# Turning the last block's frames on VectorE through memory, and loading and turning the second block's frames earlier

## The chip, the cores and the metric

The kernel runs on one core of one Trainium2 chip. The metric is the device time of one execution in microseconds (us); a kernel's time is the median of several executions. A core has TensorE (PE; its weight loads are PEld), VectorE (DVE), ScalarE (ACT), GpSimd (POOL) and SyncE (SP). SP and POOL issue most transfers between memory and the on-chip buffers, each in the order of its own queue. All engines work through their lists in order; semaphores make one wait for another.

## The reference

One inference step of a streaming encoder with one layer. There are 2048 prompt frames and 32 sample frames, 2080 in all, of width 1024.

```python
hn = rmsnorm(h, g_mix)
proj = hn @ w_in                       # 1024 -> 3072: hA, bA, cA, zA, vB, zB of 512 each
u = cA * hA                            # mixer A: causal convolution of width 3
yA = bA * (conv3(u) + conv_b) * silu(zA)
# mixer B: 4 groups of 128 channels, trailing mean over 2/4/8/16 frames minus the frame
yB = (pooled @ pool_w) * pool_scale * silu(zB)
h = h + concat[yA, yB] @ w_out
h = h + (p @ w_ple) * sigmoid(rmsnorm(h, g_ple) @ w_ple_gate)
y = rmsnorm(h, g_final)                # and the last frames of u and v as states
```

Everything is float32. The kernel splits each factor of a product into a high and a low part in a shorter format and adds three products of parts (high x high, high x low, low x high).

## The kernel before, in words

**Blocks and groups.** The 2080 frames are five blocks of 416 (`NB`), in `GROUPS = [[0, 1], [2, 3], [4]]`. A block has four columns of frames: three of 128 and one of 32. `w_in`'s product needs the frames turned, that is channels on partitions and frames along the row. To get there each column of 128 frames is loaded as rows (`x_load`, on SP, into the ring `xin` of five buffers), its squares are summed on ScalarE (`x_stat`, `sumsq`), the root is taken on POOL, VectorE scales it by the root and by `g_mix` (`normal`, one instruction of 128x1024), TensorE turns it in eight 128x128 pieces, four to a bank (`turn`), and `put`/`split` reads the bank twice: a cast on ScalarE gives the high part, a subtraction on VectorE the low part.

**The beginning.** Block 0 is loaded, turned and split first, into `B0["11"]` and `B0["21"]` (the halves of the channels). Its short column and block 1's are loaded together as `short0`. The weights of the first three products, `zb`, `v` and `c` of the first unit, are loaded and split ahead (`first_w`). Then the generator `second` (`second_block`) does block 1 step by step: three steps that load, sum and scale a column each, four that turn a column, split it into `B0["12"]` and `B0["22"]` and copy the turned frames back over the column's rows (`both`), and four that build sums and differences of the two blocks. The first unit's `Unit.plain` takes these steps between its products: `zb`, `v`, `c` of block 0, then `zb`, `v`, `c` of block 1, then `h`, `za`, `b`. Between them a small product `pm` (`mix`, three matmuls) reads `pw`, the split pooling weights. A turn `pv` puts small vectors (convolution weights, histories, `g_ple`) from `rows` into `vec`; in before it stands ahead of the units. `project` runs a product of 24 matmuls of 128x416, two halves of 12.

**Units 1 to 7.** From the second unit on, two blocks are multiplied together by a scheme of seven block products in place of eight (`Unit.seven`, `pair`): seven steps of 12 matmuls for each of three pairs of weights (`zb`/`v`, `c`/`h`, `za`/`b`). Weights come by SP into `raws` (four buffers) and are split by ScalarE and VectorE into `wr` (seven tiles), ahead of TensorE. During group 0 the generator `next_columns` prepares group 1's frames and writes them to memory (`p_d`). During group 1, from its second unit on, the generator `last_block` prepares block 4: it is taken one step in three calls of `aside`, and there is a call for each step of a pair. Its split frames go through `staged` tiles in `xin` to memory (`b_d`, written by POOL) and are loaded as `hn[4]` at the start of group 2.

**After that.** Group 2 multiplies block 4 plainly. Then come the output projection (`h_d`) and the gate with the final norm, in the same scheme of seven. The gate stage already turns frames on VectorE: `blocks` reads rows of `h_d` so that a 32x32 block transpose over the whole tile (`turned_here`) finishes the turn, and `turned_here`'s result is read through a rearranged view.

**Order.** The list of each engine is set by a scheduler that may move an instruction; `tc.keep_in_program_order` holds one where the program has it. Tiles of a pool are handed out in turn, and a new tile waits until the old one's readers are done. `bank` has six PSUM banks, `tbank` two.

Of the kernel before, what the change touches and what calls it, by code (L numbers as in the profile page):

```python
# [34 lines left out]
def trunk(ctx, tc, x_p, x_s, c_conv, c_pool, p_p, p_s, g_mix, w_in, conv_w, conv_b, pool_w,  # L35
# [19 lines left out]
    def tbank(name):  # L55
        return ps_t.tile([P, 512], F32, tag="tr", name=name)
# [19 lines left out]
    def split(hi, lo, src, eng=nc.vector):  # L76
        ins = nc.scalar.copy(hi, src)  # L77
        eng.tensor_tensor(lo, src, hi.bitcast(F32), op=ALU.subtract)
        return ins
# [227 lines left out]
    def ring4(t, name):  # L307
        return t.tile([P, D], F32, tag="t", name=name)
# [21 lines left out]
    with ExitStack() as s1:  # L330
# [21 lines left out]
        def ftile(name):  # L352
            return wk.tile([P, KH, P], F32, tag="f", bufs=4, name=name)
# [47 lines left out]
        def x_tile(name, rows):  # L401
            return x_stat(x_load(name, rows))

        def normal(x):
            xt, n, r = x
            nc.vector.scalar_tensor_tensor(xt[:n], xt[:n], r[:n], g_bc[:n], op0=ALU.mult, op1=ALU.mult)  # L406

        def turn(x, half, name, get=tbank, later=False):
            xt, n, _ = x
            pt = get(name)  # L410
            for k in range(KH):
                kk = half * KH + k
                ins = nc.tensor.transpose(pt[:, k * P:k * P + n], xt[:n, kk * P:(kk + 1) * P], ident[:n, :n])
# [143 lines left out]
        def half_product(ps, lhs, b, start, stop=True):  # L557

            for k in range(KH):
                for q, (x, y) in enumerate(((0, 0), (0, 1), (1, 0))):  # L560
                    nc.tensor.matmul(ps[:, :NB], lhs[:, k, x], b[:, k, y], start=start and k + q == 0,  # L561
                                     stop=stop and k == KH - 1 and q == 2, skip_group_check=True)

        begun = []

        def project(ps, w, tb):
            x = hn[tb]
            if begun:
                for half in range(2):
                    half_product(ps, w[half], x[half], half == 0, half == 1)  # L570
                return

            begun.append(tb)
            steps = sorted(((k, a, b) for k in range(KC) for a, b in ((0, 0), (0, 1), (1, 0))), key=lambda t: t[1:])
# [12 lines left out]
            for half, q in enumerate(("11", "21")):  # L587
                put(B0[q][:, :, :, c * P:c * P + n], turn(x, half, f"pt0_{c}_{half}", bank)[:, :, :n])
        hn[0] = B0["11"], B0["21"]
        first_w.extend([weights(kind, 0, f"first{kind}") for kind in ("zb", "v", "c")])  # L590
        B0["12"] = piece_of(seventh("B0_12"), 0)
        hn[1] = B0["12"], B0["22"]

        def second_block():

            spans = [(c, slice(c * P, min(NB, c * P + P))) for c in range(4)]
            xs = []
            for c in range(3):
                x = x_tile(f"1_{c}", [x_rows(1, c)])
                normal(x)  # L600
                xs.append((x, slice(0, P)))
                yield
            xs.append((short0, slice(DEC, 2 * DEC)))
            both = []
            for c, cs in spans:
                x, ts = xs[c]
                n = ts.stop - ts.start
                both.append([x[0][:, half * NH:half * NH + KH * n].rearrange("p (k t) -> p k t", k=KH)
                             for half in range(2)])
                for half, q in enumerate(("12", "22")):  # L610
                    pt = turn(x, half, f"pt1_{c}_{half}", bank)[:, :, ts]
                    put(B0[q][:, :, :, cs], pt)
                    nc.scalar.copy(both[c][half], pt)
# [19 lines left out]
        second = second_block()  # L633


        rows = ftile("rows").rearrange("p k n -> p (k n)")[:112, :P]
        nc.gpsimd.memset(rows, 0.0)
        nc.sync.dma_start(rows[0:12], conv_w[0].rearrange("r (j c) -> (r j) c", c=P))
# [2 lines left out]
        nc.sync.dma_start(rows[32:40], c_conv[0, 0].rearrange("r (j c) -> (r j) c", c=P))  # L641
        nc.sync.dma_start(rows[40:100], c_pool[0, 0].rearrange("r (j c) -> (r j) c", c=P))
        nc.sync.dma_start(rows[100:108].rearrange("k (q c) -> k q c", q=4), g_ple[0].rearrange("(q k c) -> k q c", q=4, k=KC))
        pv = tbank("pv")
        nc.tensor.transpose(pv[:, :112], rows, ident[:112, :112])
        vec = const.tile([P, 112], F32, name="vec")
        nc.vector.tensor_copy(vec, pv[:, :112])
        cw = lambda r, j: vec[:, r * 4 + j:r * 4 + j + 1]
        cb = lambda j: vec[:, 12 + j:13 + j]
        pscale = lambda j: vec[:, 16 + j:17 + j]  # L650
        hist_u = lambda j: vec[:, 32:40].rearrange("p (r j) -> p r j", j=4)[:, :, j]
        hist_v = lambda j: vec[:, 40:100].rearrange("p (r j) -> p r j", j=4)[:, :, j]

        pw = one.tile([P, 2, 4, P], F32R, name="pw")
        pw_raw = raws.tile([P, 4, P], F32, tag="t", name="raw_pw")
        nc.sync.dma_start(pw_raw, pool_w[0].rearrange("g c d -> c g d"))
        split(pw[:, 0], pw[:, 1], pw_raw)

        def etile(name, n=NB):
            return wk.tile([P, 2 * NB + 16], F32, tag="e", bufs=2, name=name)[:, :n]  # L660
# [1 line left out]
        class Unit:  # L662
# [98 lines left out]
            def plain(self):  # L761
                tbs, j, tag, zs, V, U, c_s = self.tbs, self.j, self.tag, self.zs, self.V, self.U, self.c_s
                blocks = range(len(tbs))

                def product_of(kind, b, w):
                    ps = bank(f"{kind}{tag}_{tbs[b]}")
                    project(ps, w, tbs[b])
                    return ps[:, :NB]

                def zb_block(b):  # L770
# [5 lines left out]
                        nc.scalar.copy(self.place(V, 15, seg), ps[:, seg[0] - o:seg[1] - o])  # L776
                    self.pool_blocks(b)

                def c_block(b):
                    nc.scalar.copy(self.cols(c_s, b), product_of("c", b, wc))  # L780

                wz, wv = weights("zb", j, f"zb{tag}"), weights("v", j, f"v{tag}")
                if len(tbs) > 1:

                    wc = weights("c", j, f"c{tag}")
                    for b in blocks:
                        zb_block(b)
                        if b == 0:
                            for _ in range(2):
                                next(second)  # L790
                        v_block(b)
                        if b:
                            self.mix(b - 1)
                            next(second)
                        else:
                            for _ in range(2):
                                next(second)
                        c_block(b)
                        if b == 0:
                            for _ in range(3):  # L800
# [242 lines left out]
        def last_block():  # L1043

            load_ahead(2, 0)
            for c in range(4):
                x = x_stat(ahead.pop((2, c))[0], True)
                if c < 3:
                    load_ahead(2, c + 1)
                normal(x)  # L1050
                yield
                for half in range(2):
                    pt = turn(x, half, f"pt4_{c}_{half}", later=True)
                    to_memory(b_d[:, half * KH:half * KH + KH], f"b_4_{c}_{half}", pt, c * P, x[1])
                    yield

        def at_pace(steps, num, den):

# [485 lines left out]
```

## Time and profile before

| what | before |
|---|---|
| runs (us) | 933.43, 933.67, 933.95; median 933.67 |
| the profiled execution (us) | 933.61 |
| its span, first to last instruction (us) | 931.8 |
| TensorE busy | 910.5 us, 98% |
| VectorE busy | 718.9 us, 77% |
| ScalarE busy | 475.3 us, 51% |
| POOL busy | 147.1 us, 16% |
| granted TensorE clock | 0.996 |

A row of a timeline has the start in us from the span's start, the duration in us, the engine, the line of the kernel, the operation, what is written from what, and in brackets how long the engine had been idle and who released it. A row with x12 stands for twelve instructions, and its duration reaches from the first's start to the last's end. Matmuls overlap, so start to start is the measure of what one costs. In a row of a group stand the busy time, the mean of one instruction in ns, and the idle time before. A row of the waits says who waited for whom, in total, how often, and the longest.

### The profile page before, as it was taken

The page shows a single profiled execution, that of the slowest core. Times are in us where ns is not written, and L with a number is a line of the kernel's source. Part 1 is how long each engine was busy: PE and PEld are TensorE (multiplying, and loading weights), DVE is VectorE, ACT ScalarE, POOL GpSimd, SP SyncE. Part 2 cuts the span into 40 slices and gives each one's busy share as a digit, 9 for nine tenths or more (in the row PEclk, how much of TensorE's full clock was granted, in tenths as well). Part 3 has the DMA queues.
Part 4 walks back from the last instruction along what each step waited for, and adds up shares of the span by engine and source line. Part 5 has one row for each costly group of instructions (what it writes and reads, how often), then busy time and mean ns, then how long its engine had stood idle before and what let it go on. Part 6 is the DMA issues. An engine that isn't in the chain of part 4 may idle for free. (4 is left out here: it accounts for less than half of the span.)

```text
span 931.8 us, 12938 instructions
## 1 busy us (share of the span) xinstructions
PE 910.5 (98%) x4511; PEld 821.3 (88%) x4511; DVE 718.9 (77%) x1209; ACT 475.3 (51%) x880; POOL 147.1 (16%) x272
## 2 busy tenths in 40 slices
PE   7999999999999999999999999999999999999996
PEld 5899998999999999999999987888877868888884
DVE  6896898899588978685777588766554798888865
ACT  5744555564445554443554356434424875565554
POOL 2210222212000110000000011111111002323334
PEclk9999999999999999999999999999999999999999
DMA  8255555759954645428655349765784885899892
GB/s 253 75 153 152 166 161 175 239 160 305 417 166 137 182 147 158 139 59 283 200 168 176 119 162 315 265 204 153 244 231 156 304 276 140 199 225 232 211 255 92
DMA packets 138254, 182.96 MB, mean 196 GB/s; under 512 B 11724, under 2 KB 109260, under 8 KB 136909
## 3 DMA queue, kind: packets, MB, share of 16 engines
q1 hardware_dynamic: 118173, 124.36, 43.5%
q0 software_dynamic: 17280, 52.27, 19.4%
q10 hardware_dynamic: 2736, 5.51, 1.8%
q8 instruction: 35, 0.57, 0.3%
q14 instruction: 30, 0.25, 0.1%
HBM read 127.23 MB, written 54.86 MB: 195 GB/s over the span
## 5 line engine op out<-in xcount | busy, mean ns | idle before, releaser
L77 ACT CAST y_S<-y_fS 128x512 fp32r<-128x512 f32 x32 | 19.5, 621 | 41.7 <-PE x_o L167 17.5
L102 PE MATMUL e<-wq,pps 128*128 128x512 f32 (+1 forms) x156 | 38.9, 400 | 0.2 <-ACT pps L77 0.2
L406 DVE SCALAR_TENSOR_TENSOR xt<-xt,rstd_x,g_bc 128x1024 f32<-128x1024 f32 (+2 forms) x18 | 23.1, 1282 | 17.0 <-POOL rstd_x L73 17.0
L167 PE MATMUL x_o<-wo_b,y_S 128*128 128x512 f32 x128 | 35.8, 391 | 0.0
L167 PE MATMUL x_g<-wg_b,g_S 128*128 128x512 f32 x128 | 35.7, 389 | 0.0
L561 PE MATMUL x_ch<-B,w_ch_S 128*128 128x416 f32 x168 | 34.6, 352 | 0.4 <-ACT c_s L859 0.4
L561 PE MATMUL x_zab<-B,w_zab_S 128*128 128x416 f32 x168 | 34.4, 352 | 0.3 <-ACT V L859 0.3
L561 PE MATMUL x_zbv<-B,w_zbv_S 128*128 128x416 f32 x168 | 34.4, 353 | 0.0
L561 PE MATMUL z_ch<-B,w_ch_S 128*128 128x416 f32 x168 | 34.1, 351 | 0.0
L561 PE MATMUL z_zbv<-B,w_zbv_S 128*128 128x416 f32 x168 | 34.1, 351 | 0.0
L561 PE MATMUL z_zab<-B,w_zab_S 128*128 128x416 f32 x168 | 34.0, 351 | 0.0
L102 PEld LDWEIGHTS e<-wq,pps 128*128 128x128 f32 (+1 forms) x156 | 27.4, 182 | 7.0 <-ACT pps L77 0.5
L1333 POOL DMA_DIRECT2D e<-h_d x28 | 24.8, 907 | 53.3 <-DVE e L1330 40.4
L561 PEld LDWEIGHTS x_zab<-B,w_zab_S 128*128 128x128 f32 x168 | 31.3, 188 | 1.0 <-ACT V L859 0.7
L561 PEld LDWEIGHTS x_ch<-B,w_ch_S 128*128 128x128 f32 x168 | 31.2, 188 | 1.0 <-ACT c_s L859 0.7
L561 PEld LDWEIGHTS x_zbv<-B,w_zbv_S 128*128 128x128 f32 x168 | 31.1, 188 | 0.8 <-ACT zs L859 0.4
L561 PEld LDWEIGHTS z_zab<-B,w_zab_S 128*128 128x128 f32 x168 | 31.4, 188 | 0.3
L561 PEld LDWEIGHTS z_ch<-B,w_ch_S 128*128 128x128 f32 x168 | 31.3, 188 | 0.4
L561 PEld LDWEIGHTS z_zbv<-B,w_zbv_S 128*128 128x128 f32 x168 | 31.3, 188 | 0.3
L77 ACT CAST y<-y 128x512 fp32r<-128x512 f32 x24 | 14.8, 618 | 29.2 <-PE x_o L167 14.0
L167 PEld LDWEIGHTS x_o<-wo_b,y_S 128*128 128x128 f32 x128 | 24.0, 188 | 5.1 <-ACT c_o L1136 0.3
L167 PEld LDWEIGHTS x_g<-wg_b,g_S 128*128 128x128 f32 x128 | 24.0, 188 | 5.0
(579 smaller groups left out, 2633.6 us busy)
## 6 DMA issues: line engine op xcount, KB each, us to landing
y<-y_d SPq DMA_DIRECT2D x16, 512.0 KB, 12.2
x<-in_x_prompt_dram SPq DMA_DIRECT2D x16, 512.0 KB, 4.9
h_d<-x SPq DMA_DIRECT2D x16, 512.0 KB, 4.5
hn<-h_d SPq DMA_DIRECT2D x61, 128.0 KB, 6.8
xt<-in_x_prompt_dram SPq DMA_DIRECT2D x15, 512.0 KB, 6.5
e<-e_d SPq DMA_DIRECT2D x15, 512.0 KB, 6.8
e<-h_d POOLq DMA_DIRECT2D x28, 256.0 KB, 6.9
out_dram<-e POOLq DMA_DIRECT2D x14, 512.0 KB, 4.2
```

Source lines behind the costliest of these rows:

```text
L77: ins = nc.scalar.copy(hi, src)
L102: nc.tensor.matmul(ps[:n], pps[:, a, k, :n], wp[k][b][:, cs], start=k + q == 0, stop=k == 1 and q == 2)
L167: nc.tensor.matmul(ps[:n], lhs[:, k, a, :n], w[b][:, k], start=start and k + q == 0, stop=k == KH - 1 and q == 2, skip_group_check=True)
L406: nc.vector.scalar_tensor_tensor(xt[:n], xt[:n], r[:n], g_bc[:n], op0=ALU.mult, op1=ALU.mult)
L561: nc.tensor.matmul(ps[:, :NB], lhs[:, k, x], b[:, k, y], start=start and k + q == 0, stop=stop and k == KH - 1 and q == 2, skip_group_chec ...
L1333: nc.gpsimd.dma_start(ee, h_d[r:r + P, at[1] * NH:at[1] * NH + NH], accum_op=ALU.add)
```

## The change

It has two parts.

*The last block.* `normal` and the turns of `last_block` on TensorE go. `scaled_to_memory` scales a column in four instructions of 256 elements, which also lay the channels out by 32, into another tile of `xin`, and POOL writes that to a new buffer in memory, `xs_d`. `from_memory` reads it back with four transfers on SP so that 32x32 blocks are all that is left to turn, and `turned_in_place` turns them on VectorE. The halves are split and written to `b_d` as before. A column's reads are issued a step after its write, and its splits follow behind the next column's scaling. There are 18 steps for 12.

*The beginning.* The loads of block 1's three columns move up between the first weights: column 0 behind `v`'s, columns 1 and 2 behind `c`'s. Their sums of squares and scalings become one step, taken before `rows` is loaded. The turns of the short column, column 0 and column 1 come behind the second product `v`, then `pv` and the split of `pw` (`vectors`), and column 2 is turned between the two halves of the third product `c`. Block 1's `c` no longer has a step ahead of it but behind the small product.

```diff
-        def normal(x):
+        def normal(x, later=False):
             xt, n, r = x
-            nc.vector.scalar_tensor_tensor(xt[:n], xt[:n], r[:n], g_bc[:n], op0=ALU.mult, op1=ALU.mult)
+            ins = nc.vector.scalar_tensor_tensor(xt[:n], xt[:n], r[:n], g_bc[:n], op0=ALU.mult, op1=ALU.mult)
+            if later:
+                tc.keep_in_program_order(ins)
...
-        def project(ps, w, tb):
+        def project(ps, w, tb, between=None):
...
                 for half in range(2):
                     half_product(ps, w[half], x[half], half == 0, half == 1)
+                    if between and not half:
+                        between()
...
-        first_w.extend([weights(kind, 0, f"first{kind}") for kind in ("zb", "v", "c")])
+        ahead1 = []
+        made = []
+        for kind, cs in (("zb", ()), ("v", (0,)), ("c", (1, 2))):
+            made.append(weights(kind, 0, f"first{kind}"))
+            ahead1.extend(x_load(f"1_{c}", [x_rows(1, c)]) for c in cs)
+        first_w.extend(made)
...
         def second_block():
...
-            xs = []
-            for c in range(3):
-                x = x_tile(f"1_{c}", [x_rows(1, c)])
-                normal(x)
-                xs.append((x, slice(0, P)))
-                yield
+            xs = [(x_stat(x, True), slice(0, P)) for x in ahead1]
+            for x, _ in xs:
+                normal(x, True)
             xs.append((short0, slice(DEC, 2 * DEC)))
-            both = []
-            for c, cs in spans:
+            yield
+            both = {}
+            for c, cs in [spans[3], *spans[:3]]:
...
-                    pt = turn(x, half, f"pt1_{c}_{half}", bank)[:, :, ts]
+                    pt = turn(x, half, f"pt1_{c}_{half}", bank, later=True)[:, :, ts]
...
         second = second_block()
+        next(second)
...
-        pv = tbank("pv")
-        nc.tensor.transpose(pv[:, :112], rows, ident[:112, :112])
-        vec = const.tile([P, 112], F32, name="vec")
-        nc.vector.tensor_copy(vec, pv[:, :112])
+
+        def vectors():
+            pv = tbank("pv")
+            tc.keep_in_program_order(nc.tensor.transpose(pv[:, :112], rows, ident[:112, :112]))
+            nc.vector.tensor_copy(vec, pv[:, :112])
+            split(pw[:, 0], pw[:, 1], pw_raw)
...
-        split(pw[:, 0], pw[:, 1], pw_raw)
...
-                def c_block(b):
-                    nc.scalar.copy(self.cols(c_s, b), product_of("c", b, wc))
+                def c_block(b, between=None):
+                    nc.scalar.copy(self.cols(c_s, b), product_of("c", b, wc, between))
...
                     for b in blocks:
                         zb_block(b)
-                        if b == 0:
-                            for _ in range(2):
-                                next(second)
                         v_block(b)
                         if b:
                             self.mix(b - 1)
                             next(second)
+                            c_block(b)
                         else:
-                            for _ in range(2):
-                                next(second)
-                        c_block(b)
-                        if b == 0:
                             for _ in range(3):
                                 next(second)
+                            vectors()
+                            c_block(b, lambda: next(second))
...
         def last_block():
             load_ahead(2, 0)
-            for c in range(4):
+            back = {}
+
+            def scale(c):
                 x = x_stat(ahead.pop((2, c))[0], True)
                 if c < 3:
                     load_ahead(2, c + 1)
-                normal(x)
+                scaled_to_memory(x, c * P)
+                return x[1]
+
+            def halves_to_memory(c, n):
+                u = turned_in_place(back.pop(c))
+                for half in range(2):
+                    t = staged(f"b_4_{c}_{half}")[:, :, :, :n]
+                    v = lambda h: t[:, :, h].rearrange("p k (g t) -> p k g t", t=32)
+                    tc.keep_in_program_order(split(v(0), v(1), u[:, half * KH:half * KH + KH]))
+                    nc.gpsimd.dma_start(b_d[:, half * KH:half * KH + KH, :, c * P:c * P + n], t.bitcast(F32))
+                    yield
+
+            for c in range(5):
+                n = scale(c) if c < 4 else 0
                 yield
-                for half in range(2):
-                    pt = turn(x, half, f"pt4_{c}_{half}", later=True)
-                    to_memory(b_d[:, half * KH:half * KH + KH], f"b_4_{c}_{half}", pt, c * P, x[1])
-                    yield
+                if c:
+                    yield from halves_to_memory(c - 1, m)
+                if n:
+                    back[c], m = from_memory(c * P, n), n
+                yield
+
+        xs_d = tc.dram_tile([NB, D], F32, name="xs_d")
+
+        def scaled_to_memory(x, r):
+            xt, n, rs = x
+            t = ring4(xin, f"xs_{r}")
+            v = lambda a, q: a[:n].rearrange("p (k q c) -> p q k c", q=4, c=32)[:, q]
+            for q in range(4):
+                o = t[:n, q * 256:q * 256 + 256].rearrange("p (k c) -> p k c", c=32)
+                tc.keep_in_program_order(nc.vector.scalar_tensor_tensor(o, v(xt, q), rs[:n], v(g_bc, q),
+                                                                        op0=ALU.mult, op1=ALU.mult))
+            nc.gpsimd.dma_start(xs_d[r:r + n], t[:n])
+
+        def from_memory(r, n):
+            t = ring4(xin, f"xb_{r}")[:, :n * KC]
+            for q in range(4):
+                nc.sync.dma_start(t[q * 32:q * 32 + 32].rearrange("p (g c) -> p g c", c=256),
+                                  xs_d[r:r + n, q * 256:q * 256 + 256].rearrange("(g p) c -> p g c", p=32))
+            return t
+
+        def turned_in_place(t):
+            tc.keep_in_program_order(nc.vector.transpose(t, t))
+            return t.rearrange("p (g k t) -> p k g t", k=KC, t=32)
```

More of the change, by code (lines that the diff above doesn't have):

```diff
@@ L596, in second_block @@
             spans = [(c, slice(c * P, min(NB, c * P + P))) for c in range(4)]
-            xs = []
-            for c in range(3):
-                x = x_tile(f"1_{c}", [x_rows(1, c)])
-                normal(x)
-                xs.append((x, slice(0, P)))
-                yield
+            xs = [(x_stat(x, True), slice(0, P)) for x in ahead1]
+            for x, _ in xs:
+                normal(x, True)
             xs.append((short0, slice(DEC, 2 * DEC)))
-            both = []
-            for c, cs in spans:
+            yield
+            both = {}
+            for c, cs in [spans[3], *spans[:3]]:
                 x, ts = xs[c]
                 n = ts.stop - ts.start
-                both.append([x[0][:, half * NH:half * NH + KH * n].rearrange("p (k t) -> p k t", k=KH)
-                             for half in range(2)])
+                both[c] = [x[0][:, half * NH:half * NH + KH * n].rearrange("p (k t) -> p k t", k=KH)
+                           for half in range(2)]
                 for half, q in enumerate(("12", "22")):
-                    pt = turn(x, half, f"pt1_{c}_{half}", bank)[:, :, ts]
+                    pt = turn(x, half, f"pt1_{c}_{half}", bank, later=True)[:, :, ts]
                     put(B0[q][:, :, :, cs], pt)
@@ L633, in trunk @@
         second = second_block()
+        next(second)
+        vec = const.tile([P, 112], F32, name="vec")
+        pw = one.tile([P, 2, 4, P], F32R, name="pw")
         rows = ftile("rows").rearrange("p k n -> p (k n)")[:112, :P]
@@ L652, in trunk @@
         hist_v = lambda j: vec[:, 40:100].rearrange("p (r j) -> p r j", j=4)[:, :, j]
-        pw = one.tile([P, 2, 4, P], F32R, name="pw")
         pw_raw = raws.tile([P, 4, P], F32, tag="t", name="raw_pw")
         nc.sync.dma_start(pw_raw, pool_w[0].rearrange("g c d -> c g d"))
-        split(pw[:, 0], pw[:, 1], pw_raw)
         def etile(name, n=NB):
@@ L763, in plain, with product_of @@
                 blocks = range(len(tbs))
-                def product_of(kind, b, w):
+                def product_of(kind, b, w, between=None):
                     ps = bank(f"{kind}{tag}_{tbs[b]}")
-                    project(ps, w, tbs[b])
+                    project(ps, w, tbs[b], between)
                     return ps[:, :NB]
```

## The prediction

> **What bounds the kernel now.** I read the page's busy times first, then who made TensorE wait, then windows around the two places that the change touches.
>
> ```profile
> span 931.8 us, 12938 instructions
> ...
> PE 910.5 (98%) x4511; PEld 821.3 (88%) x4511; DVE 718.9 (77%) x1209; ACT 475.3 (51%) x880; POOL 147.1 (16%) x272
> ```
>
> ```profile
> PE pt L413 <- DVE xt L406: 2.9, 2, 2.3
> ...
> PE zb L561 <- ACT B L77: 1.7, 1, 1.7
> ```
>
> ```profile
> 0.00:16.00 16.00, 9.46 (x36) 5.72 (x36) 8.85 (x13) 9.71 (x18) 5.48 (x45) 1.00 0.86 227
> 16.00:38.00 22.00, 20.18 (x111) 19.05 (x112) 18.08 (x32) 15.05 (x33) 3.61 (x6) 0.92 0.60 172
> 38.00:52.00 14.00, 14.00 (x76) 13.86 (x76) 13.64 (x26) 10.13 (x21) 1.06 (x1) 1.00 0.18 54
> 100.00:200.00 100.00, 97.17 (x525) 93.89 (x524) 90.04 (x150) 55.26 (x105) 24.52 (x31) 1.00 0.62 187
> 285.00:390.00 105.00, 105.00 (x568) 102.77 (x568) 86.84 (x143) 51.35 (x93) 11.09 (x16) 1.00 0.53 155
> ```
>
> The columns are PE, PEld, DVE, ACT and POOL busy time, then granted clock, DMA share and GB/s. TensorE is busy 910.5 of 931.8 us and waits for almost nothing by name, so the kernel is TensorE's own list of instructions plus its few stands: what leaves that list, or what ends a stand, shortens the run one for one. From 285 to 390, where the last block is turned, TensorE is busy throughout and VectorE idle for 18.2 of 105 us. The beginning has one stand, 1.7 us before the second block's first product.
>
> **The last block's turns leave TensorE.**
>
> ```profile
> 293.69 2.43 PE L561 MATMUL x_zbv<-B,w_zbv_S 128*128 128x416 f32 x12
> 295.97 0.60 PE L413 MATMUL pt<-ident,xt 128*128 128x128 f32 x4
> 296.32 2.52 PE L561 MATMUL z_zbv<-B,w_zbv_S 128*128 128x416 f32 x12
> 298.68 2.43 PE L561 MATMUL x_zbv<-B_T,w_zbv 128*128 128x416 f32 x12
> 300.95 0.60 PE L413 MATMUL pt<-ident,xt 128*128 128x128 f32 x4
> ...
> 359.53 0.43 PE L413 MATMUL pt<-ident,xt 32*128 32x32 f32 x4
> ```
>
> Start to start, twelve matmuls take 2.27 us (298.68 to 300.95). From 293.69 to 298.68 there are 24 of them and four turns: 4.99 - 4.54 = 0.45 us for a group of four (0.35 to the next start, 0.1 on the product after it). Eight such groups, the first and last shown, go: 8 x 0.45 = **3.6 us**, the short ones at the same price, since a few columns less change little. Nothing else on TensorE hides them.
>
> What replaces them goes to VectorE and to the queues:
>
> ```profile
> L406 DVE SCALAR_TENSOR_TENSOR xt<-xt,rstd_x,g_bc 128x1024 f32<-128x1024 f32 (+2 forms) x18 | 23.1, 1282 | 17.0 <-POOL rstd_x L73 17.0
> ```
> ```profile
> 29.17 0.58 DVE L746 SCALAR_TENSOR_TENSOR pl<-win,V 128x415 f32<-128x415 f32 x1
> ```
> ```profile
> L1310 DVE STREAM_TRANSPOSE hn<-hn 128x1024 f32<-128x1024 f32 x15 | 18.6, 1239 | 5.1 <-DMA hn<-h_d 5.1
> L78 DVE TENSOR_TENSOR g<-hn,g 128x512 fp32r<-128x512 f32 x22 | 14.9, 683 | 0.3
> ```
>
> The scaling of a column, one instruction of 1.28 us, becomes four over 256 elements. By the line through 1024 (1.28) and 415 (0.58) one takes 0.40, four 1.6; if time went with length alone, 1.28. I take 1.6: +0.3 a column, +1.3 for four. Three whole turns at 1.24 (the kernel has this form already, in its last stage) and one of 256 elements, by the same slope 0.4, add 4.1. The eight splits now read turned frames in memory on chip rather than a bank; the nearest row, 683 ns for such a source, is the old price. Together **+5.4 us on VectorE** against 18.2 us idle there: it hides. If that idle time were not to be had, TensorE would lose up to 5.4 us.
>
> The new wait is the trip through memory. VectorE's program order puts the first turn behind the pool split `pp`, at 307.8 of before, the scale at 292.81:
>
> ```profile
> 292.81 1.28 DVE L406 SCALAR_TENSOR_TENSOR xt<-xt,rstd_x,g_bc 128x1024 f32<-128x1024 f32 x1 [0.73 <-POOL rstd_x L73]
> ...
> 306.81 1.01 DVE L78 TENSOR_TENSOR pp<-pl,pp 128x832 fp32r<-128x832 f32 x1
> ```
> ```profile
> DMA to landing us min/median/max: 3.1/4.9/10.7
> ```
> ```profile
> hn<-h_d SPq DMA_DIRECT2D x61, 128.0 KB, 6.8
> ```
> ```profile
> 300.25 0.37 SPq L511 DMA_DIRECT2D raw_zbv_2a<-in_w_in_dram  x1
> ```
> ```profile
> 321.46 1.76 PE L561 MATMUL y_zab<-B,w_zab 128*128 128x416 f32 x8
> ```
>
> The nearest writes are those of `b_d` from POOL (3.1/4.9/10.7 us), the nearest reads those of `h_d` in the same pattern, 6.8. The median trip is 11.7 us from 294.4, so 306.1; even 10.7 + 6.8 gives 311.9, a stand of 4 us. Behind the turn on VectorE stands the split of `w_zab`'s second quarter, which TensorE reads at 321.46: a cover of 13 us, for `wr` holds seven weight tiles. So the wait costs 0. The later turns stand 15 us or more behind their reads in VectorE's order, and what the last of them feeds is read only in the third group.
>
> On SP the reads stand ahead of `raw_zbv_2a`, issued at 300.25, and wait for the write, at about 299.5: the load goes out some 2 us later, with 17 us until its split. The sixteen reads are 6 us of issue on a queue that is mostly empty. The later loads of `g_fin` and of the first `y` tiles wait longer, but their readers come 60 us on. On POOL four more writes, 0.9 us each by the rows of `b_d`, delay only the next root of a column. All told 3.4 MB more traffic over 105 us, 32 GB/s beside 155.
>
> By the Trainium skill, page "DMA: Bandwidth & Descriptors", section "Anatomy of one DMA", a transfer costs about 2.0 us plus its bytes over 436 GB/s, an estimate of 3.2 us for 512 KB and 6.4 for the trip; the rows say nearly twice that, and the sum is the same with both. The Trainium skill's page "VectorE: DVE Perf Modes", section "Rules for kernel authors", gives a 128x128 turn to TensorE where a result in its banks will do. That speaks against the change; by it the sum would be that of rival (b), and the windows row of 285 to 390 is why I take the other.
>
> **The beginning.**
>
> ```profile
> 22.58 4.51 PE L561 MATMUL v<-B,w_firstv 128*128 128x416 f32 x23
> 26.92 1.04 PE L413 MATMUL pt<-ident,xt 128*128 128x128 f32 x8
> 27.71 4.78 PE L561 MATMUL c<-B,w_firstc 128*128 128x416 f32 x24
> 32.33 2.55 PE L413 MATMUL pt<-ident,xt 128*128 128x128 f32 x24
> 34.80 0.46 PE L712 MATMUL pm<-pp,pw 128*128 128x416 f32 x1
> ...
> 37.37 0.45 PE L561 MATMUL zb<-B,w_firstzb 128*128 128x416 f32 x1 [1.74 <-ACT B L77]
> ```
> ```profile
> 27.12 0.51 ACT L776 COPY V<-v 128x416 f32<-128x416 f32 x1 [1.61 <-PE v L561]
> ...
> 28.57 1.06 ACT L77 CAST B<-pt 128x512 fp32r<-128x512 f32 x2
> ...
> 32.62 1.18 ACT L613 COPY xt<-pt 128x512 f32<-128x512 f32 x2 [1.70 <-DVE B L78]
> ```
>
> Before, three columns are turned behind the third product `c`, and ScalarE (0.53 a cast, 0.59 a copy) and VectorE then need until 37.37 to split them. After, short column, columns 0 and 1 are turned behind the second product `v`, column 2 between the halves of `c`. TensorE's work up to `zb` is the same but for `pm`, which moves behind `v` of the second block, 0.5 us: 26.7 + 3.3 of turns + 0.2 `pv` (which has left the first product, hence 26.7) + 4.6 for `c` + 0.1 for one more break = 34.9. Two waits remain. `c` takes the bank of the first short turn, free once ScalarE has done V, two short casts (0.25 each), `pw` (0.62), one cast and the copy: 27.4 + 0.5 + 0.62 + 0.53 + 0.3 = 29.4, against TensorE's 29.2. And `zb` needs column 2 split: from 29.4 ScalarE has eight casts and copies, `pp` and `w_h` (about 5.4 us) up to column 2's first cast, 34.8, and VectorE 0.65 after it: 35.5. So `zb` starts at about 35.5, and 37.4 - 35.5 - 0.5 = **1.4 us** are won. Bounds: 2.0 with no stand at all, 0 if ScalarE's list comes 1.4 us later than I add up.
>
> It could come later through memory. The frames' loads move up: column 0 ahead of `firstc`, columns 1 and 2 behind it. At the 227 GB/s of the first 16 us the 5.0 MB up to column 2 are there at about 24; its square then still precedes `V<-v`. `rows` and `pw` fall behind them, `pw` to about 26, and its cast on ScalarE is due at 27.9: a cover of 2 us, the thinnest here. If that is gone, `c` slips by as much. `vec`, `pw` and `w_h` move back on VectorE, which was full from 38 to 52 (13.64 of 14): its three scalings, done sooner, buy it about what `w_h` costs later, and I count that `w_h` is split 0.3 us ahead of the product that needs it.
>
> **Sum.** The profiled execution took 933.61 us (span 931.8 and 1.8 around it), the median is 933.67, so they are one. 933.6 - 3.6 - 1.4 = **928.6**.
>
> **Rivals.**
> (a) The beginning gives nothing: ScalarE's list or `pw`'s landing keeps `zb` at 37, or the next stage takes it back (from 100 to 200 VectorE is 90% busy and TensorE loses 2.8 us, which could grow by what comes sooner). For it speaks the exact balance above; against it that TensorE's reach at 34.9 has half a microsecond to spare. 933.6 - 3.6 = 930.0.
> (b) VectorE's 5.4 us are not hidden, its idle time being waits that the order cannot fill: half of it lost, 933.6 - 3.6 - 1.4 + 2.7 = 931.3.
> (c) Slower: the first trip through memory outlasts VectorE's place for it. VectorE is in order and everything behind the turn stands. It decides from a trip of 13 + 13 = 26 us on, twice the row's; at 38 us TensorE would lose 12, and the time would be 940. Against it: SP is empty at that place and the reads go out alone.
> (d) The change does not move the turns: the program order shows it does, TensorE's list loses eight groups; no chance worth naming.
>
> **How the numbers follow.** Forecast 0.62 (its own range 927.6 to 929.6: the beginning between 2.0 and 0.7 and a few tenths either way); (a) 0.2; (b) 0.09; (c) 0.06; 0.03 for more than I see. The range takes in (a) and most of (b): 927.4 to 931.4. A measurement tells 0.2% (1.9 us) from no change: faster, that is under 931.8, 0.62 + 0.2 + 0.05 + 0.03 = 0.9; within it 0.04; slower 0.06.
>
> **What would show it.** Right: no `pt` turns on TensorE past 40 us; `x_zbv` to `z_zbv` starts 2.27 apart from 285 on; four STREAM_TRANSPOSE on `xb` with idle time before them under 5 us in all; `zb` of the second block starting at 35.5 with under 0.7 us of wait; the stage from 100 to 200 still at about 2.8 us idle on TensorE. Wrong: TensorE waiting for `w_zab` or `w_zbv` casts between 300 and 390, `c` waiting more than a microsecond for ScalarE, or the stands from 150 to 162 grown by what the beginning won.

## The result, and the profile after

After took 928.27 us (median of 6, 927.2 to 928.9), before 933.81 over 6 runs: a ratio of 0.994, 95% interval 0.9927 to 0.9953. In a later comparison after took 927.69 (e11, below) against 933.16, ratio 0.9936 [0.9915, 0.9957]. The forecast was 928.6 with a range of 927.4 to 931.4. The profiled execution of after took 928.9 us.

The page of after and its list of waits, who waited for whom (total, times, longest):

```profile
span 927.1 us, 12920 instructions
...
PE 906.4 (98%) x4479; PEld 817.4 (88%) x4479; DVE 722.5 (78%) x1225; ACT 475.7 (51%) x880; POOL 153.1 (17%) x276
```
```profile
PE pt L415 <- DVE xt L406: 2.3, 1, 2.3
PE pt_g L415 <- DVE xt L406: 1.8, 2, 1.2
PE x_ch L563 <- ACT c_s L866: 1.2, 1, 1.2
...
PE c L563 <- ACT xt L620: 0.5, 1, 0.5
```

The 32 turns are gone from TensorE's count (4511 to 4479) and the wait of `zb` is gone from the list; `c` has one of 0.5 us in its place. Three of the prediction's windows, columns as there:

```profile
16.00:38.00 22.00, 21.46 (x128) 20.46 (x127) 19.84 (x36) 17.49 (x37) 5.85 (x6) 1.00 0.46 133
100.00:200.00 100.00, 95.98 (x519) 92.78 (x518) 88.89 (x148) 53.88 (x101) 23.43 (x30) 1.00 0.61 186
285.00:390.00 105.00, 104.70 (x555) 103.29 (x554) 92.23 (x159) 53.75 (x97) 13.32 (x20) 1.00 0.56 165
```

From 285 to 390 VectorE shows 92.23 us for 86.84, but that window doesn't hold the same work in both: after reaches 285 with 2 us more done, and 390 with over 5. The stretch from the start of the second unit of group 1 to the start of group 2 does hold the same work. Before, then after:

```profile
284.63:434.77 150.14, 150.14 (x807) 147.44 (x807) 120.52 (x195) 70.99 (x127) 12.20 (x18) 1.00 0.50 153
```
```profile
282.50:429.24 146.74, 146.44 (x775) 144.60 (x775) 124.52 (x211) 71.56 (x127) 14.44 (x22) 1.00 0.59 180
```

TensorE has the 32 turns less (807 to 775 matmuls) and is done 3.40 us sooner; VectorE has 16 instructions more (twelve scalings, four turns) and is 4.0 us busier. From 16 to 38 the granted clock is 1.00, where before had 0.92. From 100 to 200 TensorE is idle for 4.0 us, where before was for 2.8.

The last block in after's timeline of TensorE, and the instructions on `xb` and `xs` (first and last start, durations as minimum, median, maximum):

```profile
291.57 2.43 PE L563 MATMUL x_zbv<-B,w_zbv_S 128*128 128x416 f32 x12
293.83 2.43 PE L563 MATMUL z_zbv<-B,w_zbv_S 128*128 128x416 f32 x12
296.10 2.43 PE L563 MATMUL x_zbv<-B_T,w_zbv 128*128 128x416 f32 x12
...
329.42 2.53 PE L563 MATMUL x_zab<-B_T,w_zab 128*128 128x416 f32 x12 [0.30 <-DVE U L869]
```
```profile
L1103 DVE STREAM_TRANSPOSE xb<-xb x4: 435/1235/1239, 304.7 to 381.3; 128x1024 f32<-128x1024 f32 x3, 128x256 f32<-128x256 f32 x1
its engine sat idle before it (us, times) until:
  DVE xs L1089: 1.0, 1
  DVE xb L1103: 0.5, 1
```
```profile
L1089 DVE SCALAR_TENSOR_TENSOR xs<-xt,rstd_x,g_bc x16: 447/477/486, 290.7 to 358.1; 128x256 f32<-128x256 f32 x12, 32x256 f32<-32x256 f32 x4
```

Twelve matmuls follow twelve at 2.27 us with nothing between them. The turns on VectorE cost 1.24 us each (the short one 0.44). A scaling of 256 elements lasts 0.48, but the next one starts before it ends: twelve of them keep VectorE busy for 5.0 us, 0.42 each. None of the turns had a transfer to wait for: the frames scaled at 290.7 to 292.4 were turned at 304.7. One stand of 0.30 us, for VectorE's `U`, is all that TensorE lost in this stretch.

The beginning in TensorE's timeline:

```profile
15.67 1.78 PE L580 MATMUL zb<-B,w_firstzb 128*128 128x416 f32 x8
...
25.00 2.60 PE L415 MATMUL pt<-ident,xt 64*128 64x64 f32 x24
27.44 0.26 PE L657 MATMUL pv<-ident,rows 112*128 112x112 f32 x1
28.23 2.53 PE L563 MATMUL c<-B,w_firstc 128*128 128x416 f32 x12 [0.54 <-ACT xt L620]
...
33.75 4.70 PE L563 MATMUL zb<-B,w_firstzb 128*128 128x416 f32 x24
...
48.48 9.22 PE L563 MATMUL h<-B,w_h 128*128 128x416 f32 x48
```

The second block's `zb` starts at 33.75 without a wait, where before had it at 37.37 behind 1.74 us. `h` starts at 48.48; in before's execution it started at 51.76. Those 3.3 us are more than the 1.4 of the forecast, and from 100 to 200 1.2 us seem to be given back. The experiments had to say whether both belong to the change.

### The profile page after: what moved, and what is told of

Read it like the earlier page. It is cut to its first block, busy times and chain, and to the rows that moved or that the text cites. A ratio compares the mean times of both kernels' runs of the same rounds, so it can differ in the third digit from the quotient of the medians.

```text
span 927.1 us, 12920 instructions
## 1 busy us (share of the span) xinstructions
PE 906.4 (98%) x4479; PEld 817.4 (88%) x4479; DVE 722.5 (78%) x1225; ACT 475.7 (51%) x880; POOL 153.1 (17%) x276
## 5 line engine op out<-in xcount | busy, mean ns | idle before, releaser
L69 POOL TENSOR_SCALAR ms_x<-ssq_x 128x1 f32<-128x1 f32 (+2 forms) x18 | 12.8, 710 | 143.9 <-ACT junk L88 143.6
L77 ACT CAST g_S<-g_fS 128x512 fp32r<-128x512 f32 x32 | 19.0, 618 | 19.0 <-DVE g_fS L1501 12.3
```

The source lines that it names most:

```text
L69: nc.gpsimd.tensor_scalar(ms[:n], ssq[:n], scalar1=1.0 / D, scalar2=EPS, op0=ALU.mult, op1=ALU.add)
```

## The experiments

The theory from these two traces: the last block brings 3.6 us; the beginning brings 1.5 from `zb`'s stand and 1.8 because block 0's first products run at the full clock, and 1.2 of it is lost again between 100 and 200. The rival: the low clock of before and the stands of after from 100 to 200 are chance in one execution, and the beginning is worth what was forecast. The kernels ran beside before in three sets, each on one chip: e1 to e4 (before's median there 933.75), e5, e6, e7 and e9 (933.68), and e8, e10, e11 and e12 (933.16).

### The two parts apart

e1 is before with `last_block` and its helpers from after; e2 is after with `last_block` from before.

> The last block's part alone, on the beginning of before. Theory (the two parts add up, and the last block's is the larger): 32 turns leave TensorE for 3.6 us and nothing is given back, so 930.2 against 933.8; TensorE idle from 285 to 390 stays under 0.5 us, and zb of the second block still waits 1.7 us near 37. Rival (the beginning carries the change, and the last block's part loses some of its 3.6 us to VectorE): 931.5 or more. The granted clock between 16 and 38 us: if the low value of before (0.92) belongs to the order of before's beginning it shows again here, as this kernel begins in the same way; if it was chance in one execution it may be 1.00.

> The beginning's part alone, with the last block of before. Theory: h of the first unit starts 3.3 us sooner than in before (1.5 from the stand ahead of zb, 1.8 from block 0's turns and first product), 1.2 of it is given back between 100 and 200 us, so 931.8 and the granted clock of 16 to 38 us is 1.00. Rival (all of it is given back): 933.3 to 933.8. Rival (the give-back between 100 and 200 belongs to the last block's part): 930.5.

e1 took 929.91 us, ratio 0.9956 [0.9938, 0.9973], 3.8 us under before. e2 took 931.56, ratio 0.9974 [0.9959, 0.9989], 2.2 under before. Together 6.0, against 5.5 for after: the parts add up within what the intervals tell. e2's time is near its theory's 931.8, but not by the theory's terms, as the traces show. TensorE's first products in before, then e1's and e2's timelines of the beginning, the start of the second unit of group 1 and the start of group 2:

```profile
16.08 3.11 PE L576 MATMUL zb<-B,w_firstzb 128*128 128x416 f32 x8
```
```profile
15.61 1.79 PE L576 MATMUL zb<-B,w_firstzb 128*128 128x416 f32 x8
...
20.59 4.51 PE L561 MATMUL v<-B,w_firstv 128*128 128x416 f32 x23
...
35.40 0.45 PE L561 MATMUL zb<-B,w_firstzb 128*128 128x416 f32 x1 [1.74 <-ACT B L77]
...
49.78 9.22 PE L561 MATMUL h<-B,w_h 128*128 128x416 f32 x48
...
282.44 2.43 PE L561 MATMUL x_zbv<-B,w_zbv 128*128 128x416 f32 x12
...
429.18 4.69 PE L561 MATMUL zb<-hn,w_zb 128*128 128x416 f32 x24
```
```profile
33.67 4.70 PE L563 MATMUL zb<-B,w_firstzb 128*128 128x416 f32 x24
...
48.41 9.22 PE L563 MATMUL h<-B,w_h 128*128 128x416 f32 x48
...
281.03 2.43 PE L563 MATMUL x_zbv<-B,w_zbv 128*128 128x416 f32 x12
...
431.16 4.70 PE L563 MATMUL zb<-hn,w_zb 128*128 128x416 f32 x24
```

e1 begins with the instructions of before, and yet reaches `h` at 49.78 and not at 51.76. Of these 1.98 us, 0.47 are there at the first `zb` (15.61 for 16.08); the other 1.5 come in the products up to `v` (20.59 for 22.58), where before's clock was low and e1's was 1.00. So these instructions alone don't bring the low clock: it came in two executions that begin with before's products (before's own and e3's, below) and not in e1's. Between two executions without it (e1 and e2) the new beginning brings `h` forward by 1.37 us and the second unit of group 1 by 1.41. The stretch from there to group 2 takes 146.74 us in e1 and 150.13 in e2, a difference of 3.39: that is the last block's part. Before and after show the same two lengths, 150.14 and 146.74, and every other execution with the last block's part and no further edit there has 146.74 too (e6, e7, e9, e11, e12):

```profile
284.63 2.43 PE L561 MATMUL x_zbv<-B,w_zbv 128*128 128x416 f32 x12
...
434.77 4.70 PE L561 MATMUL zb<-hn,w_zb 128*128 128x416 f32 x24
```
```profile
282.50 2.43 PE L563 MATMUL x_zbv<-B,w_zbv 128*128 128x416 f32 x12
...
429.24 4.70 PE L563 MATMUL zb<-hn,w_zb 128*128 128x416 f32 x24
```

From 100 to 200 TensorE was idle for 2.6 us in e2, which has after's beginning. From `h` to the second unit of group 1 e2 took 232.62 us, e1 232.66 and before 232.87, so nothing of the beginning's gain is given back there; the 234.02 of after, with its 4.0 us idle, was chance as well.

### The order of the loads alone

```diff
-        first_w.extend([weights(kind, 0, f"first{kind}") for kind in ("zb", "v", "c")])
+        for kind, cs in (("zb", ()), ("v", (0,)), ("c", (1, 2))):
+            made.append(weights(kind, 0, f"first{kind}"))
+            ahead1.extend(x_load(f"1_{c}", [x_rows(1, c)]) for c in cs)
+        first_w.extend(made)
...
-                x = x_tile(f"1_{c}", [x_rows(1, c)])
+                x = x_stat(ahead1[c])
```

> Before with one thing changed: the loads of the second block's three columns stand between the first weights, as in after; their sums, scalings and turns stay where they are in before. Theory (the order of the loads alone lets the third column of block 0 land 1.6 us sooner, so that its turns run without a stand and the clock stays at 1.00): v of block 0 starts near 20.6 as in after, in place of 22.6, and zb of the second block at 35.5 to 37.4, its stand not shorter than 1.7; 932 to 933.5. Rival (the placing of the turns brings the sooner start, by pv and the vector rows leaving the first product): v of block 0 starts at 22.4 and the time is 933.8.

934.35 us, ratio 1.0005 [0.9991, 1.0019]: nothing. Its execution had the same stands as before's ahead of 16 us and the same low clock, with the loads in the new order, so the order doesn't cure it. `v` of block 0 started at 22.37, as the rival had it. The theory's account of the load order falls.

e7 is the other half: after, with the three loads behind all first weights.

> After, with the loads of the second block's three columns behind all three first weights instead of between them; the turns stay where after has them. Theory (the placing of the turns carries the beginning's gain and the loads come early enough either way): column 1's scaling moves by under 1 us, h starts at 48.5 to 49.2, 928.3 to 929.0. Rival (the turns behind v need the loads ahead of firstc): TensorE waits 1 to 2 us at pt behind v, h at 50, 929.7 or more.

927.47 us, ratio 0.9927 [0.9908, 0.9946]. `c` waited 0.51 us as in after, and `h` started at 48.83. The gain of the beginning is in where the turns stand, with the scalings ahead of them; the early loads are not needed for it. The time is under the 928.3 to 929.0 that was expected, and `h` within its range.

### VectorE with three times the turns

```diff
-            tc.keep_in_program_order(nc.vector.transpose(t, t))
+            for _ in range(3):
+                tc.keep_in_program_order(nc.vector.transpose(t, t))
```

> After, with each of the last block's four turns on VectorE done three times in the same place (an odd number leaves the same frames): 2 x (3 x 1.24 + 0.44) = 8.3 us more on VectorE between 285 and 390, where 12.8 us are idle. Theory (VectorE's idle time there can be filled, so the 5.4 us of after are hidden with room to spare): within 0.5 us of after, 928.3 to 928.8. Rival (half of VectorE's added time reaches TensorE): 932.4.

928.17 us, as after. The stretch from the second unit of group 1 to group 2:

```profile
281.52:428.59 147.07, 146.71 (x776) 144.53 (x775) 130.95 (x219) 70.25 (x127) 14.56 (x22) 1.00 0.59 179
```

VectorE has the eight turns more (219 instructions for 211) and is 6.4 us busier than in after. The stretch is 0.33 us longer, so TensorE lost a twentieth of that. VectorE's idle time could be filled, which was the step that rival (b) doubted.

### A longer trip through memory

```diff
             nc.gpsimd.dma_start(xs_d[r:r + n], t[:n])
+            if r == 0:
+                for i in range(HOPS):          # HOPS = 5, hop[0] = xs_d[0:P]
+                    nc.gpsimd.dma_start(hop[i + 1], hop[i])
...
-                                  xs_d[r:r + n, q * 256:q * 256 + 256]...
+                                  (hop[HOPS] if r == 0 else xs_d[r:r + n])[:, q * 256:q * 256 + 256]...
```

> After, with the first column of the last block passing through memory five times more (five copies of 512 KB from memory to memory, each waiting for the one before, issued by POOL) before SP reads it: the trip grows from 10 us to some 25 to 35. In the instruction lists VectorE then has some twenty other instructions ahead of the first turn. Theory (the trip is hidden by place, since what is turned is not needed on TensorE before the third group): within 1 us of after, 928 to 929.3. Rival (the forecast's slower case, VectorE or SP stands in order behind the late column): TensorE stands for 7 us or more between 300 and 350, 935 or more.

930.23 us, ratio 0.9968 [0.9952, 0.9984], 2.5 more than after beside it (e11). In e8 the first turn starts at 322.6, 31 us behind the issue of the column's write at 291.5; in after it starts at 304.7, 12 us behind a write at 292.7. TensorE's timeline, POOL's, ScalarE's, and the turns:

```profile
321.02 2.43 PE L563 MATMUL z_zab<-B,w_zab_S 128*128 128x416 f32 x12
325.89 2.54 PE L563 MATMUL x_zab<-B,w_zab_S 128*128 128x416 f32 x12 [2.44 <-ACT V L866]
```
```profile
291.52 0.60 POOL L1093 DMA_DIRECT2D xs_d<-xs  x1 [2.00 <-DVE xs L1091]
...
314.29 0.49 POOL L1096 DMA_DIRECT2D hop<-hop  x1 [4.32 <-DMA hop<-hop]
```
```profile
323.86 1.14 ACT L77 CAST b<-xb 128x512 fp32r<-128x512 f32 x2 [4.23 <-DVE xb L1108]
...
325.36 0.48 ACT L866 COPY V<-x_zab 128x416 f32<-128x416 f32 x1
```
```profile
L1108 DVE STREAM_TRANSPOSE xb<-xb x4: 432/1240/1245, 322.6 to 382.9; 128x1024 f32<-128x1024 f32 x3, 128x256 f32<-128x256 f32 x1
```

Neither side was right. The trip is not free at any length: with the turn 19 us later TensorE stood 2.44 us for a copy of `V`, and the stretch to group 2 is 2.7 longer (149.41 us). The copy was late because ScalarE, in order too, had two casts of the turned frames ahead of it, which waited 4.23 us for the turn. That it cost no more goes with VectorE's list in e8, which has other work ahead of the late turn; what so late a column would cost in after's own order isn't shown. The mechanism of rival (c) exists, by way of ScalarE, and at 31 us it took 2.4; I had put its start at 26 us and its price at 12 for 38. In after nothing waited for the trip.

### The low clock and the stands

e5 (on before) and e6 (on after) put ten spare turns ahead of block 0's short column; e10 is e5 with sixteen more ahead of the second block's `zb`.

```diff
             normal(x)
+            if c == 3:
+                spare = tbank("spare")
+                for i in range(10):
+                    tc.keep_in_program_order(nc.tensor.transpose(spare[:, i % 4 * P:i % 4 * P + P], ident, ident))
```

> Before, with ten spare 128x128 turns of the unit matrix on TensorE (their result is read by nobody) ahead of the turns of block 0's short column, where before's execution stood 1.33 us and then ran its first twelve matmuls at a granted clock of 0.54 and 0.61. Theory (the low clock follows the stands between 12 and 15.3 us, which come where block 0's third column lands late): the clock of 16 to 20 us is 1.00, h starts at 49.8 to 50.2 as in the execution of the last block's part alone, and the median falls by a share of the 2 us, since not every execution has the stands: 932.0 to 933.3. Rival (the low clock does not follow the stands): 933.8 to 934.4, and it may still show 0.54 there.

> After, with the same ten spare turns in the same place. Theory (none of the three executions profiled with this beginning had the low clock, so that there is little to win): 928.0 to 928.8, h at 48.5 to 49.0. Rival (the low clock comes in many executions of after too): 927.3 or less.

> Before, with spare turns in both of its early stands: ten ahead of block 0's short column and sixteen (1.85 us) ahead of the second block's zb. Theory (the clock is lowered once for some 3 us behind a stand of TensorE over 1.3 us; with one stand filled it came behind the other): 1.00 in every window up to 52 us, h at 49.6 to 50.2 and a lower median, 931.5 to 932.7. Rival (the low clock does not follow the stands): it shows again before 52 us, 933.7.

e5 took 933.68 us, e10 933.23, both the time of before (ratios 0.9999 [0.9978, 1.0021] and 0.9995 [0.9983, 1.0007]). e6 took 931.03, ratio 0.9964 [0.9948, 0.998], worse than after. All three missed the medians of their theories. Windows of 2 us, of before and then of e5, and two longer ones of e10 (the clock is the third number from the end):

```profile
16.00:18.00 2.00, 1.92 (x6) 1.86 (x7) 2.00 (x6) 2.00 (x6) 0.00 (x0) 0.54 0.76 185
18.00:20.00 2.00, 2.00 (x8) 1.95 (x7) 2.00 (x4) 1.39 (x3) 0.00 (x0) 0.61 1.00 397
```
```profile
36.00:38.00 2.00, 2.00 (x9) 1.85 (x8) 1.82 (x4) 2.00 (x7) 0.00 (x0) 0.70 0.31 104
38.00:40.00 2.00, 2.00 (x7) 1.93 (x7) 1.92 (x4) 0.07 (x1) 0.00 (x0) 0.50 0.03 7
```
```profile
16.00:38.00 22.00, 21.40 (x134) 20.51 (x133) 19.33 (x35) 16.47 (x37) 3.62 (x6) 1.00 0.56 166
38.00:52.00 14.00, 14.00 (x75) 13.85 (x75) 14.00 (x25) 8.48 (x17) 1.91 (x2) 1.00 0.32 96
```

In e5's execution the clock was full at 16 to 20 us, and it then fell behind the next stand, the 1.73 us ahead of `zb`; `h` started at 51.55. With both stands filled (e10) it was 1.00 up to 52 us and `h` started at 50.31, still 0.5 later than in e1, which had a full clock without spare turns. And e10's median is no lower than before's. So that the low clock follows stands has support, in single executions, and that it is worth anything in the median has none: its share in the 2.2 us of e2 stays open. Also open is why e6 lost 2.8 us to after (and 3.6 to e7 in its own set), of which its execution shows 0.44 at `h` and a stand of 1.99 at 575 us where after's has 0.41.

### After again, and a faster version

e9 moves the sums of squares of group 1's columns, in `next_columns`:

```diff
                     if after is not None and i in (6, 7):
                         load_half_ahead(after)
+                    if after is not None and i == 9:
+                        ahead[(1, after)] = [x_stat(x, True) for x in ahead[(1, after)]]
```

and `frame_sums` doesn't take them again for those columns. e12 is e9 with e7's order of loads.

> After, with one step of the next group's frames moved: the sums of squares of a pair of columns are taken in the last step of the pair before, a step sooner, and the step they leave is empty. In every kernel so far four turns at 155 wait 1.16 us for VectorE's scaling and four more 0.62, and x_ch ahead of them up to 1.2 for a copy of c_s that stands behind a sum of squares on ScalarE. Theory (the scaling is late because the sums are taken late): these stands go, TensorE's idle time from 100 to 200 falls from 2.6 to 4.0 down to 1 us, 926.3 to 926.8. Rival (another wait takes their place, the loads of the columns or the next copy): 928.0 to 928.6.

> After itself once more, beside the others. Theory (after has no early stand over 1.3 us, so no low clock, and what its executions differ in is later waits for loads): granted clock 1.00 up to 52 us, h at 48.4 to 49.0, 927.5 to 929. Rival (the 931.0 of after with spare turns is what after takes on some chips): 930 or more.

> After with both changes that did not hurt: the sums of squares one step sooner (927.2 alone) and the second block's loads behind the first weights (927.5 alone). Theory (the first wins the stands near 155, the second is worth nothing either way): 926.8 to 927.4, at least 0.8 under after in the same call. Rival (the gain of the first was chance): the same as after within 0.3.

e9 took 927.18 us, ratio 0.9918 [0.9898, 0.9939], between its theory and its rival; after itself didn't run in that set, and e7 took 927.47 there. e11 took 927.69, as its theory had it, though with a low clock later on. e12 took 925.72, ratio 0.9909 [0.9889, 0.9928], 2.0 us under after in the same set, better than expected and the fastest version here. The stands of after (e11's execution), then what is left of them in e12, in TensorE's timeline; then the stage in e12's windows:

```profile
154.80 0.63 PE L415 MATMUL pt_g<-ident,xt 128*128 128x128 f32 x4 [1.17 <-DVE xt L406]
...
156.80 1.09 PE L415 MATMUL pt_g<-ident,xt 128*128 128x128 f32 x4 [0.61 <-DVE xt L406]
...
158.72 3.12 PE L563 MATMUL z_ch<-B,w_ch_S 128*128 128x416 f32 x12
```
```profile
153.50 0.63 PE L415 MATMUL pt_g<-ident,xt 128*128 128x128 f32 x4 [0.49 <-DVE xt L406]
```
```profile
100.00:200.00 100.00, 99.19 (x543) 96.78 (x542) 92.04 (x152) 57.38 (x109) 26.88 (x31) 1.00 0.66 196
```

TensorE's idle time from 100 to 200 fell to 0.8 us, in e9 as in e12. From `h` to the second unit of group 1 they took 230.3 and 230.2 us, where the seven executions with after's beginning and without this edit took 232.4 to 234.0: the move alone is worth 2.1 us or more there, and the order of the loads has no part in it. What stood there was the time from the sum of squares by way of the root to the scaling, with too little room between them, in before as in after.

## Why the prediction was right, step by step

**The last block: right in its steps, with VectorE's price put too high.** Forecast 3.6 us; the stretch from the second unit of group 1 to group 2 became 3.40 shorter, that is 3.70 for the turns less the stand of 0.30 at 329.42. VectorE's +5.4 came out at 4.0 over the same work. Its rows fit the forecast: the scalings take 6.7 us for 5.1 (+1.6, forecast 1.3) and the turns 4.1, as forecast. That busy time rose by less than these 5.7 is probably closer packing, since an instruction that follows at once overlaps the one before and the overlap counts once (a split of 0.68 us is followed 0.60 later); no run tests that. It was hidden, and e4 shows that 6 us more would be, but for 0.33. The trip through memory was put at 11.7 us. The writes landed after 3.0 us and the reads after 5.3 (medians), 8.3 together, and the turn, which started 12.0 us behind the issue of the write, waited for nothing.

**The beginning: right in size, wrong in its clock times.** Forecast 1.4 us; between executions alike in their clock (e1 and e2) it is 1.37 at `h` and 1.41 at the second unit of group 1. But `zb` came at 33.7 without a wait, not at 35.5 with up to 0.7. What was off is the end of `v`: I took 26.7 from an execution whose first matmuls ran at a granted clock of 0.54 and 0.61, and I had quoted its row in the windows (0.92) without using it. In after `v` ends at 25.0. Those 1.7 us cancel in the forecast of 1.4, since 37.4 and 35.5 both carry them; without them the forecast for `zb` is 33.8. Of the two waits, `c`'s was 0.5 and not 0.2, and `zb`'s was none and not 0.6: the delay came a step sooner, with the same end.

**The loads.** I gave the new order of loads a part in the gain and named `pw`'s landing as the thinnest cover. The order did nothing, alone (e3) or taken away (e7), and `pw` did not hold `c`.

**Rival (a)** looked true in after's first execution, with 4.0 us idle from 100 to 200 for 2.8. In e11, the same kernel, it was 1.9 us, and from `h` to the second unit of group 1 e11 took 232.93 us, its low clock included, for before's 232.87: nothing was given back. One execution's stands of a microsecond are no evidence either way in this kernel.

**The sum** 928.6 came within 0.4 of the first median and 0.9 of the second. The parts make 4.8 us in the traces (1.4 and 3.4) where the medians fell by 5.5; the interval takes in both, and the 0.7 between them is not placed. The sum made against before's execution held although that execution was 2.2 us behind e1's at 285 us (284.63 against 282.44), 1.5 of it by the low clock: after's had about 1.4 us of stands more than e2's from 100 to 200, and 0.8 more behind the start of group 2 (497.03 us in before, 497.86 in after). That both came out near their medians was luck of the two profiles.

## What to carry to other kernels

Where TensorE is busy 98% of the time, count what leaves its list and price it start to start: 32 turns were worth 3.4 us net, and the 4 us that VectorE took over cost TensorE 0.3 because the window of that stage, not the share of the whole span, showed room. Compare stretches that hold the same work, from one named instruction to another, and not equal times of the clock. Before a difference of a microsecond or two between two traces is explained, look at the granted clock of the windows and at a second execution: the two parts run apart gave two more executions of the same stretches and told chance from change. Between a chain's steps that are called at a pace (sum of squares, root, scaling, turn), one step more of distance can be worth as much as a change of the work itself: 2.1 us or more here.

## What the runs showed of the hardware

The granted clock of TensorE was lowered to 0.50 in four executions, each time behind a stand: at 16 us behind 1.33 (before and e3), near 37 behind 1.73 (e5), and near 157 in e11 behind 1.17 and 0.61, where twelve matmuls took 3.12 us instead of 2.43. In windows of 1 us the share that is missing adds up to 1.71 us in each of the four, that is half the clock for 3.4 us. It made TensorE 1.5 to 1.6 us later (before and e5 against e1, e11 against e2). Behind the same stands the clock stayed at 1.00 in e1 (1.74 at 35.4) and, near 155, in after, and it stayed so behind longer ones: 1.99 in e6, 2.44 in e8. The Trainium skill, page "TensorE: Matmul & The Clock Gate", section "HAM oscillation — how this bites in real kernels", puts the rule at idle gaps above about 3.4 us. Here gaps of a third to half of that were enough at times, so the measurement decides: short stands carry a risk of about 1.6 us each, not a certain cost.

SP's issue of one transfer took 5.19 us in before (the load of `firstc` at 4.96) and 3.88 in after (the first column of the second block at 4.85), where most take 0.3 to 0.5. It was the ninth transfer in SP's list in each of the fourteen executions (3.88 to 5.25 us), whichever of the two loads stood there, so the wait goes with the place in the queue and not with the transfer.
